# FoX attention scores by two full-height matmuls, and a projection step between the probability transposes and the value product

## The chip, the core and the metric

The kernel runs on one core of a Trainium2 chip. The time is the device time of one execution in microseconds; the median of three timed runs of the kernel before is 1479.12 us (1475.91 to 1482.52). The engines are TensorE (PE in the profile, its weight loads are PEld), VectorE (DVE), ScalarE (ACT), GpSimd (POOL) and SyncE (SP), which issues the transfers. TensorE's results go to PSUM, eight banks of 512 float32 columns on 128 partitions.

## The reference

One decoder layer on 512 tokens of width 1024, in float32: a SwiGLU half-step, a token mixer of two branches side by side, and a second SwiGLU half-step, each between norms and scaled by vectors made from a conditioning input. The change lies in the mixer's second branch, forgetting attention (FoX), with 16 heads of 64 columns:

```
def fox_attention(q, k, v, logf):
    F = jnp.cumsum(logf, axis=-1)
    ...
    def block(args):
        qi, Fi, i = args
        s = jnp.einsum('bhqd,bhkd->bhqk', qi, k).astype(jnp.float32) * scale
        s = s + Fi[..., None] - F[:, :, None, :]
        ...
        s = jnp.where(kpos[None, :] <= qpos[:, None], s, -jnp.inf)
        p = jax.nn.softmax(s, axis=-1)
        return jnp.einsum('bhqk,bhkd->bhqd', p.astype(v.dtype), v)
```

A block has 128 queries. With 512 tokens there are four of them, and the masked scores need 1, 2, 3 and 4 tiles of 128 keys.

## The kernel before

**Products in parts.** TensorE takes float32r operands, which hold fewer bits than float32. So a matrix is split into a first part and a remainder (`hi`, `lo`), and a product is the sum of three matmuls, hi·hi, hi·lo and lo·hi, into one PSUM bank (`mm3`, L192). All projections go that way: weights are loaded in pieces of 512 KB, rounded to hi by ScalarE (L155), subtracted to lo by VectorE (L156).

**Scores.** Two heads, a pair, share the 128 partitions: head e (0 or 1) has its 64 columns on half e. For a head, `qk_parts` puts the query's first part on the head's own half `n` of a tile `qx[e]` and its remainder on the other half `o`. In `kx[e]` the key's remainder is on `n` and its first part on `o`. A 128-row matmul of `qx[e]` and `kx[e]` gives hi·lo + lo·hi at once (L748), and a 64-row matmul on half `n` alone, with the key's first part `kh`, gives hi·hi (L747). Each query tile of each head takes these two, for 128, 256, 384 or 512 keys: 16 score matmuls to a pair. VectorE adds the forget bias and the mask, which GpSimd prepares from a transferred row (L731 to L737), and takes the maximum, in one instruction per tile (L751); this also frees the score's PSUM bank.

**Softmax and turn.** `fox_soft`: negated maximum (L758), exponentials with their sums on ScalarE (L760), reciprocals (L762), normalization on VectorE (L764). `fox_out`: 20 transposes of 128 x 128 into PSUM (L776), six copies to SBUF by ScalarE (L778), eight products with the values (L784), and the split of the result into parts (L198, L199).

**What sets the order.** Attention alone would leave TensorE waiting for the softmax, so projections of later pairs stand between its parts. `Fill` holds them as steps of 12 matmuls of 512 columns; `F.run(n)` takes the next n, `F.until` all up to a mark. The loop at L841 is the plan: softmax of pair p, a step, scores of pair p + 1, the steps for pair p + 2's query and key, transposes and values of pair p (`fox_out`), `evacuate()` (the parts of pair p + 2), one more step. A scheduler then orders every engine's instructions at build time, starting from this program order, and each engine runs its own list strictly in that order. A matmul that waits therefore holds back all matmuls behind it.

**Space.** SBUF has 69 units of 2 KB a partition, shared by everything but the weights (`unit()`); a pair's parts take five of them. Of the eight PSUM banks six are for long accumulations (`acc()`: projections, scores, value products, one transposed group), two for short ones (`aux()`: the other transposes). A pair's projections hold two of the six while they run.

Of the kernel before, what the change touches and what calls it, by code (L numbers as in the profile page):

```python
# [8 lines left out]
F32 = mybir.dt.float32  # L9
F32R = mybir.dt.float32r  # L10
# [3 lines left out]
ALU = mybir.AluOpType  # L14

P = 128
# [6 lines left out]
EPS = 1e-6  # L23
# [4 lines left out]
NU = 69        # 2 KiB units per partition that everything but the weight stream shares  # L28
# [3 lines left out]
NMM = 6        # PSUM banks for long accumulations; the others for short ones  # L32
LOOK = 4       # steps that weight loads run ahead
KTAIL = 6      # last contraction tiles of a down projection, taken token tile by token tile
ROWS_A = (4, 5, 5, 4)  # of a column's 8 products in the first modulation, those off VectorE
# [4 lines left out]
def tile_hybrid_layer(  # L40
# [43 lines left out]
    @contextmanager  # L84
    def in_order(last):
        # each engine issues what the block traces in the order of the trace; last: its last instructions
        start = len(nc.cur_bb.bb.instructions)
        yield
        for i in list(nc.cur_bb.bb.instructions)[start:]:
            if i.engine in last:  # L90
                after_inst(i, last[i.engine])
            last[i.engine] = i

    @contextmanager
    def not_before(last):
        # no engine issues what the block traces before its last of those
# [62 lines left out]
    class Block:  # L159
        # rows k0*128.. and columns c0.. of a weight matrix, loaded in parts of 512 KiB  # L160
# [8 lines left out]
        def fetch(self, a=0, b=None):  # L169
            # the parts that cover rows a..b, where not on the way yet  # L170
# [31 lines left out]
    def ada_acc(src):  # L202
        # silu(c) weighted sums over each partition's 8 rows of 512 columns
# [17 lines left out]
    def ada_fetch_first(ch):  # L221
        # rows of shift and scale of the first sub-layer, in space that is free at the start
# [8 lines left out]
    def ada_sum_a(us, ks):  # L231
        # the sums of the first rows of those, on ScalarE and GpSimd
# [5 lines left out]
    def ada_sum_b(us, k0):  # L238
        # of the last, on VectorE, and of both
# [11 lines left out]
    def mod_cols(shc, scc, i, ch):  # L251
        # shift and scale of sub-layer i, 256 columns of each, one column per 128
# [26 lines left out]
    def mod_gate(g, i, h, factor):  # L279
        # factor * gate * g_post as a row on all partitions, 512 columns  # L280
# [18 lines left out]
    def rstd_of(s0, s1, width):  # L299
        # (s0 + s1) / width + EPS, to the power -1/2; s0 may be absent  # L300
# [32 lines left out]
    def x_turned(tp, xn, dp, bank=aux):  # L333
        # two normalized token tiles, columns 256*dp.., transposed
# [7 lines left out]
    def make_h(tp, hs, shc, scc):  # L342
        # two token tiles: normalize, transpose, modulate, split
# [27 lines left out]
    def gu_matmuls(ps, gw, uw, hs, ks, ts, js=range(4), late=False):  # L371
        # js: gate and up of each of the two row tiles; late: with the second parts of h last
# [8 lines left out]
    def ffn(w_gu, w_dn, hs, extra, gate, after, ps=None):  # L381
        # ps: the first block's products, where they are there already
# [56 lines left out]
    for u in xT:  # L439
        nc.gpsimd.memset(u[:, 0:1], 0.0)    # takes its place ahead of the loads below  # L440
# [3 lines left out]
    with in_order(last):  # L444
# [9 lines left out]
        def norm(t):  # L454
            # into space that is for weights later
# [16 lines left out]
        def modulated(ch, a, n):  # L472
            # ahead of this and after it, the first n and the others of the next chunk's rows
# [58 lines left out]
    class Fill:  # L532
        # projections in steps of 2.6 us of tensor engine work, in order; loads run LOOK steps ahead
# [25 lines left out]
        def nat(self, c0, evac):  # L559
            # h @ w_in[:, c0:c0+512] in natural layout, by token tile  # L560
# [573 lines left out]
```

## Time and profile before

| what | value |
|---|---|
| median of 3 timed runs | 1479.12 us (1475.91 to 1482.52) |
| span of the profiled execution, first to last instruction | 1477.1 us |
| that median less that span | 2.0 us |
| TensorE busy | 1431.9 us, 97% |
| VectorE, ScalarE, GpSimd busy | 765.0, 518.4, 204.6 us |
| attention stage, first score to last value product | about 501 to 695 us |

The page gives no time of the profiled execution other than its span; the median is 2.0 us above it. Engines work side by side, so busy shares don't add up; what matters is who is waited for. Matmuls overlap in the records (one that is listed with 0.39 us is followed by the next after 0.23), so "busy" is not "at full rate", and the price of a matmul is read from start to start. The granted clock is TensorE's: 1.00 is 2.4 GHz and 0.50 is 1.2 GHz; a value between is a stretch with both.

### The profile page before, as it was taken

To read this page: it belongs to the slowest core of one execution; us is meant where nothing else is said; L and a number is where in the kernel's file an instruction comes from. 1 tells how busy PE (TensorE), PEld (TensorE's weight loads), DVE (VectorE), ACT (ScalarE), POOL (GpSimd) and SP (SyncE) were. 2 spreads that over 40 slices of the span, in tenths; PEclk is the share of its full clock that TensorE was granted. 3 is DMA by queue.
4 is the path that set the end of the run, shared out by engine and by line. 5 is a ranking of instruction groups with operands and counts; after the bars stand their busy time and mean duration, and the time that the engine had idled before them with its cause. 6 is when DMAs were issued, how large, how long until landed. Compare 5 with 4: busy or idle time off the path is not lost.

```text
span 1477.1 us, 17043 instructions
## 1 busy us (share of the span) xinstructions
PE 1431.9 (97%) x6477; PEld 1134.2 (77%) x6477; DVE 765.0 (52%) x1210; ACT 518.4 (35%) x891; POOL 204.6 (14%) x328
## 2 busy tenths in 40 slices
PE   4899999999999999999999999999999999999998
PEld 3688888878877766767888887887878888887886
DVE  6945543462265677572544565547664334346232
ACT  5332222232154353534733343433343223222121
POOL 6200000000061633340101112100050000000001
PEclk7999999999999999999999999999999999999999
DMA  9444542272337645122242222224623322335411
GB/s 322 153 140 148 159 149 86 72 242 100 87 105 217 195 138 156 37 72 61 68 131 84 72 72 64 65 73 134 221 72 96 103 87 86 100 100 171 143 58 57
DMA packets 156462, 173.35 MB, mean 117 GB/s; under 512 B 8778, under 2 KB 123574, under 8 KB 156380
## 3 DMA queue, kind: packets, MB, share of 16 engines
q1 hardware_dynamic: 156380, 172.26, 37.9%
q8 instruction: 51, 0.84, 0.2%
q14 instruction: 31, 0.25, 0.1%
HBM read 168.00 MB, written 4.23 MB: 117 GB/s over the span
## 4 chain that ended last, share of the span: by engine, by line
PE 88%; DVE 6%; ACT 2%; issue 1%; DMA 1%; POOL 1%; SPq 0%; DVEq 0%; POOLq 0%; ACTq 0%
PE mm L192 47%; PE mm L378 32%; PE mm L784 2%; PE mm L747 2%; PE mm L748 1%; PE aux L957 1%; DVE t L213 1%; PE aux L776 1%; DVE wlo L156 1%; PE aux L268 1%; ACT jk L314 1%; DMA raw<-in_w_dn_dram 1%; POOL sm L310 1%; DMA u<-in_x_dram 0%; DVE t L243 0%
## 5 line engine op out<-in xcount | busy, mean ns | idle before, releaser
L156 DVE TENSOR_TENSOR wlo<-raw,whi 128x1024 fp32r<-128x1024 f32 x218 | 271.7, 1249 | 412.4 <-ACT whi L155 404.6
L378 PE MATMUL mm<-u,whi 128*128 128x512 f32 (+1 forms) x1472 | 451.4, 390 | 10.3 <-ACT u L198 9.9
L155 ACT CAST whi<-raw 128x1024 fp32r<-128x1024 f32 x220 | 230.3, 1050 | 543.9 <-PE mm L192 301.6
L192 PE MATMUL mm<-whi,u 128*128 128x512 f32 x1216 | 390.4, 397 | 1.5 <-ACT u L198 1.5
L378 PEld LDWEIGHTS mm<-u,whi 128*128 128x128 f32 x1472 | 274.4, 190 | 75.5 <-ACT u L198 13.1
L192 PE MATMUL mm<-u,whi 128*128 128x512 f32 x896 | 292.2, 406 | 0.8 <-DVE u L984 0.8
L378 PE MATMUL mm<-u,wlo 128*128 128x512 f32 (+1 forms) x736 | 283.4, 389 | 0.0
L192 PEld LDWEIGHTS mm<-whi,u 128*128 128x128 f32 x1216 | 228.2, 188 | 54.3 <-ACT u L198 1.7
L192 PE MATMUL mm<-wlo,u 128*128 128x512 f32 x608 | 240.3, 395 | 0.0
L192 PEld LDWEIGHTS mm<-u,whi 128*128 128x128 f32 x896 | 170.2, 192 | 44.4 <-issue 2.5
L192 PE MATMUL mm<-u,wlo 128*128 128x512 f32 x448 | 179.8, 402 | 0.0
L378 PEld LDWEIGHTS mm<-u,wlo 128*128 128x128 f32 x736 | 139.7, 190 | 31.0
L192 PEld LDWEIGHTS mm<-wlo,u 128*128 128x128 f32 x608 | 114.2, 188 | 27.9
L192 PEld LDWEIGHTS mm<-u,wlo 128*128 128x128 f32 x448 | 86.1, 192 | 20.7
L307 POOL TENSOR_SCALAR sm<-ss 128x1 f32<-128x1 f32 x12 | 2.3, 191 | 666.8 <-ACT jk L314 666.8
L198 ACT CAST u<-t 128x512 fp32r<-128x512 f32 (+1 forms) x84 | 44.5, 537 | 113.8 <-DVE t L401 78.3
L213 DVE SCALAR_TENSOR_TENSOR t<-raw,csil,t 128x512 f32<-128x512 f32 x98 | 74.4, 759 | 2.7 <-DMA raw<-in_w_ada_dram 0.7
L735 POOL TENSOR_SCALAR u<-t,Ft 128x128 f32<-128x128 f32 (+1 forms) x64 | 42.6, 676 | 105.9 <-DMA t<-Fd 76.8
L400 DVE SCALAR_TENSOR_TENSOR t<-t,mm 128x512 f32<-128x512 f32 x44 | 30.1, 684 | 47.0 <-ACT t L399 47.0
L760 ACT ACTIVATE u<-u,sm 128x128 f32<-128x128 f32 (+1 forms) x64 | 35.3, 555 | 47.8 <-DVE sm L758 47.8
L399 ACT ACTIVATE t<-mm 128x512 f32<-128x512 f32 x44 | 26.1, 594 | 63.2 <-PE mm L378 63.2
L401 DVE SCALAR_TENSOR_TENSOR t<-t,mm 128x512 f32<-128x512 f32 x44 | 30.2, 687 | 30.7 <-PE mm L378 29.0
(175 smaller groups left out, 1124.1 us busy)
## 6 DMA issues: line engine op xcount, KB each, us to landing
raw<-in_w_gu_dram SPq DMA_DIRECT2D x88, 512.0 KB, 3.8
raw<-in_w_in_dram SPq DMA_DIRECT2D x64, 512.0 KB, 3.8
raw<-in_w_dn_dram SPq DMA_DIRECT2D x44, 512.0 KB, 3.8
raw<-in_w_ada_dram SPq DMA_DIRECT2D x64, 256.0 KB, 3.1
raw<-in_w_ada_dram SPq DMA_DIRECT2D x24, 512.0 KB, 3.8
u<-in_w_ada_dram SPq DMA_DIRECT2D x32, 256.0 KB, 6.6
raw<-in_w_in_dram SPq DMA_DIRECT2D x16, 256.0 KB, 3.0
t<-Fd SPq DMA_DIRECT2D x16, 256.0 KB, 4.4
```

Source lines behind the costliest of these rows:

```text
L155: nc.scalar.copy(hi, raw)
L156: (eng or nc.vector).tensor_tensor(lo, raw, hi.bitcast(F32), ALU.subtract)
L192: nc.tensor.matmul(ps, a[i], b[j], start=first and n == 0, stop=last and n == 2)
L198: nc.scalar.copy(hi, src)
L213: nc.vector.scalar_tensor_tensor(a, raw[:, j, :], csil[:, k:k + 1], a, ALU.mult, ALU.add)
L378: nc.tensor.matmul(p_[:, ts], w_[k][i][:, cs], hs[k][e][:, ts], start=ks[0] == 0 and n == 0, stop=ks[-1] == KD - 1 and n == 3 * len(ks) - 1)
L400: nc.vector.scalar_tensor_tensor(th, th, 1.0, pg, ALU.add, ALU.mult)
L401: nc.vector.scalar_tensor_tensor(th, th, 0.5, pu, ALU.mult, ALU.mult)
L735: nc.gpsimd.tensor_scalar(s_at(s, i), fb[:, 0:n], -1.0, Ft[:, i, h:h + 1], ALU.mult, ALU.add)
L747: nc.tensor.matmul(sp[:, 0:n], qx[e][es, ts], kh[es, 0:n], start=True, stop=False)
L760: nc.scalar.activation(s_at(S[e], i), s_at(S[e], i), AF.Exp, bias=nmx[e][:, i:i + 1], accum_out=rs[e][:, i:i + 1])
L784: nc.tensor.matmul(po[64 * e:64 * e + 64, j * P:T], vb[j][h // 8][:, (h % 8) * 64:(h % 8 + 1) * 64], p_at(PT[e], j), start=j == 0, stop=j ...
```

## The change

`qk_parts` builds two key tiles for each head: `kx[e]` as before, and `ky[e]`, with the key's first part on half `n` and its remainder on half `o`. The hi·hi matmul becomes a 128-row matmul of `qx[e]` and `ky[e]`, which gives hi·hi + lo·lo. The shared 128-row copy `kh` is gone; a pair's parts take six units. On ScalarE a pair has six instructions in place of three, on VectorE six as before. `fox_out` is cut in two, `fox_turn` (transposes and copies) and `fox_out` (value products), and one step of projections, taken from those ahead of the transposes, goes between them. Comments are dropped, which moves no instruction.

```diff
             def parts(q, k):
-                qx, kx, kh = (unit(F32R), unit(F32R)), (unit(F32R), unit(F32R)), unit(F32R)
-                nc.scalar.copy(kh, k)
+                qx, ky, kx = [(unit(F32R), unit(F32R)) for _ in range(3)]
                 for e in range(2):
                     n, o = halves[e], halves[1 - e]
+                    nc.scalar.copy(ky[e][n], k[n])
+                    nc.vector.tensor_tensor(kx[e][n], k[n], ky[e][n].bitcast(F32), ALU.subtract)
                     nc.scalar.activation(qx[e][n], q[n], AF.Copy, scale=scale)
                     nc.vector.scalar_tensor_tensor(qx[e][o], q[n], scale, qx[e][n].bitcast(F32),
                                                    ALU.mult, ALU.subtract)
-                    nc.vector.tensor_tensor(kx[e][n], k[n], kh[n].bitcast(F32), ALU.subtract)
-                    nc.vector.tensor_copy(kx[e][o], kh[n])
-                dst.append((qx, kx, kh))
+                    nc.vector.tensor_copy(kx[e][o], ky[e][n])
+                    nc.scalar.copy(ky[e][o], kx[e][n])
+                dst.append((qx, ky, kx))
...
             for e in range(2):
-                es, ts = halves[e], slice(i * P, (i + 1) * P)
+                ts = slice(i * P, (i + 1) * P)
                 sp = acc()
-                nc.tensor.matmul(sp[:, 0:n], qx[e][es, ts], kh[es, 0:n], start=True, stop=False)
+                nc.tensor.matmul(sp[:, 0:n], qx[e][:, ts], ky[e][:, 0:n], start=True, stop=False)
                 nc.tensor.matmul(sp[:, 0:n], qx[e][:, ts], kx[e][:, 0:n], start=False, stop=True)
...
-    def fox_out(p, state):
+    def fox_turn(state):
         S = state[0]
         PT = []
...
             PT.append(pt)
+        return PT
+
+    def fox_out(p, PT):
         po = acc()
...
         if p < 6:
-            F.until(marks[p + 2])
-        else:
-            F.run((1, 5)[p - 6])
-        fox_out(p, st[p])
+            F.until(marks[p + 2] - 1)
+        elif p == 7:
+            F.run(4)
+        PT = fox_turn(st[p])
+        F.run(1)
+        fox_out(p, PT)
         evacuate()
```

On TensorE, the end of the third pair's turn. L776 is a transpose, L784 a value product, L192 a projection; `aux` and `mm` are PSUM banks. Before:

```order
L776 MATMUL aux_4524<-ident,u_4195 128x128
L776 MATMUL aux_4524<-ident,u_4194 128x128
L784 MATMUL mm_4547<-u_4509,u_3068 64x512
L776 MATMUL aux_4537<-ident,u_4211 128x128
L776 MATMUL aux_4537<-ident,u_4210 128x128
L776 MATMUL aux_4537<-ident,u_4209 128x128 x2
L776 MATMUL aux_4543<-ident,u_4210 128x128
L776 MATMUL aux_4543<-ident,u_4209 128x128
L784 MATMUL mm_4547<-u_4528,u_3068 64x512
L784 MATMUL mm_4547<-u_4510,u_3070 64x384
L192 MATMUL mm_4595<-u_2850,whi_4383 128x512
L784 MATMUL mm_4547<-u_4529,u_3070 64x384
```

and of the changed kernel, in which the transpose is L778 and the value product L789:

```order
L778 MATMUL aux_4322<-ident,u_3976 128x128
L778 MATMUL aux_4322<-ident,u_3975 128x128
L192 MATMUL mm_4157<-u_2860,whi_4022 128x512
L192 MATMUL mm_4157<-u_2861,whi_4022 128x512
L192 MATMUL mm_4157<-u_2860,wlo_4023 128x512
L192 MATMUL mm_4157<-u_2862,whi_4022 128x512
L192 MATMUL mm_4157<-u_2863,whi_4022 128x512
L192 MATMUL mm_4157<-u_2862,wlo_4023 128x512
L192 MATMUL mm_4157<-u_2864,whi_4022 128x512
L192 MATMUL mm_4157<-u_2865,whi_4022 128x512
L192 MATMUL mm_4157<-u_2864,wlo_4023 128x512
L789 MATMUL mm_4340<-u_4288,u_3068 64x512
```

The value products stood in three pieces, between transposes and a projection; now all eight stand together (seven more follow the last row), behind nine projections.

On TensorE, the start of the fifth pair's scores. L747 is the 64-row score matmul, L748 the 128-row one; the width is the number of keys. Before:

```order
L747 MATMUL mm_4431<-u_4341,u_4337 128x128
L192 MATMUL mm_4388<-u_2858,whi_4256 128x512
L192 MATMUL mm_4388<-u_2859,whi_4256 128x512
L192 MATMUL mm_4388<-u_2858,wlo_4257 128x512
L192 MATMUL mm_4388<-u_2860,whi_4256 128x512
L192 MATMUL mm_4388<-u_2861,whi_4256 128x512
L748 MATMUL mm_4431<-u_4339,u_4337 128x128
L747 MATMUL mm_4434<-u_4341,u_4338 128x128
L747 MATMUL mm_4439<-u_4341,u_4337 128x256
L748 MATMUL mm_4439<-u_4339,u_4337 128x256
L747 MATMUL mm_4442<-u_4341,u_4338 128x256
```

and of the changed kernel, with L749 for hi·hi + lo·lo and L750 for the cross terms:

```order
L749 MATMUL mm_4451<-u_4355,u_4353 128x128
L750 MATMUL mm_4451<-u_4357,u_4353 128x128
L192 MATMUL mm_4407<-u_2858,wlo_4193 128x512
L192 MATMUL mm_4407<-u_2860,whi_4192 128x512
L192 MATMUL mm_4407<-u_2861,whi_4192 128x512
L192 MATMUL mm_4407<-u_2860,wlo_4193 128x512
L192 MATMUL mm_4407<-u_2862,whi_4192 128x512
L192 MATMUL mm_4407<-u_2863,whi_4192 128x512
L749 MATMUL mm_4454<-u_4356,u_4354 128x128
L749 MATMUL mm_4459<-u_4355,u_4353 128x256
L750 MATMUL mm_4454<-u_4358,u_4354 128x128
L750 MATMUL mm_4459<-u_4357,u_4353 128x256
```

The order of the scores is nearly the same; the first tile's second matmul comes earlier, and in the groups that stand unbroken the order does not change at all.

On ScalarE, the copies of the third pair's transposes (L778), with the exponentials of the next pair (L760). Before:

```order
L760 ACTIVATE u_4209,sm_4221<-u_4209,sm_4220 128x512
L778 COPY u_4286<-aux_4289 128x512
L778 COPY u_4287<-aux_4295 128x512
L778 COPY u_4288<-aux_4301 128x256
L778 COPY u_4305<-mm_4308 128x512
L155 CAST whi_4465<-raw_4463 128x1024
L778 COPY u_4306<-aux_4314 128x512
L778 COPY u_4307<-aux_4320 128x256
```

and of the changed kernel, where the copy is L780 and the exponential L762:

```order
L762 ACTIVATE u_4210,sm_4221<-u_4210,sm_4220 128x512
L780 COPY u_4288<-aux_4291 128x512
L780 COPY u_4289<-aux_4297 128x512
L762 ACTIVATE u_4226,sm_4237<-u_4226,sm_4236 128x128
L780 COPY u_4290<-aux_4303 128x256
L780 COPY u_4307<-mm_4310 128x512
L780 COPY u_4308<-aux_4316 128x512
L780 COPY u_4309<-aux_4322 128x256
L762 ACTIVATE u_4227,sm_4237<-u_4227,sm_4236 128x256
```

All eight exponentials of the next pair stood ahead of the copies; now four stand ahead, one between and three behind.

## Rows read from the trace of the kernel before

**Rows 1.** The page: busy us per engine; engines' shares of the chain that ended last.

```profile
PE 1431.9 (97%) x6477; PEld 1134.2 (77%) x6477; DVE 765.0 (52%) x1210; ACT 518.4 (35%) x891; POOL 204.6 (14%) x328
...
PE 88%; DVE 6%; ACT 2%; issue 1%; DMA 1%; POOL 1%; SPq 0%; DVEq 0%; POOLq 0%; ACTq 0%
```

**Rows 2.** Stages, whole attention: us, busy per engine (instructions), PEclk, DMA, GB/s.

```profile
501.00:695.00 194.00, 193.72 (x840) 133.54 (x839) 122.26 (x324) 93.47 (x228) 65.37 (x125) 0.95 0.34 99
```

**Rows 3.** Stages: score groups 501.19, 655.73; the other rows are projections.

```profile
501.19:507.53 6.34, 6.34 (x18) 3.46 (x17) 4.49 (x15) 2.03 (x3) 6.34 (x13) 0.81 0.78 225
507.53:515.25 7.72, 7.72 (x25) 5.84 (x23) 5.36 (x11) 4.15 (x11) 5.58 (x11) 0.71 0.32 114
...
545.46:551.09 5.63, 5.63 (x26) 4.47 (x25) 5.32 (x13) 3.78 (x14) 4.97 (x6) 1.00 0.31 77
566.80:573.64 6.84, 6.84 (x24) 5.39 (x23) 6.42 (x17) 4.48 (x16) 0.00 (x0) 0.77 0.50 135
614.31:621.45 7.14, 7.14 (x25) 5.63 (x24) 3.84 (x16) 4.47 (x16) 0.00 (x0) 0.76 0.00 0
655.73:662.74 7.01, 7.01 (x17) 3.77 (x17) 4.19 (x16) 0.00 (x0) 2.94 (x5) 0.71 0.00 0
662.74:666.83 4.09, 4.09 (x14) 3.20 (x13) 1.47 (x7) 2.29 (x8) 0.00 (x0) 0.65 0.01 2
```

**Rows 4.** Timeline, TensorE, scores of the fourth pair: start us, us, instruction.

```profile
561.88 0.33 PE L748 MATMUL mm<-u,u 128*128 128x128 f32 x1
562.13 0.38 PE L747 MATMUL mm<-u,u 64*128 64x256 f32 x1
...
563.38 0.44 PE L747 MATMUL mm<-u,u 64*128 64x384 f32 x1
563.75 0.44 PE L748 MATMUL mm<-u,u 128*128 128x384 f32 x1
...
565.10 0.50 PE L747 MATMUL mm<-u,u 64*128 64x512 f32 x1
565.52 0.49 PE L748 MATMUL mm<-u,u 128*128 128x512 f32 x1
```

**Rows 5.** Timeline, TensorE, fifth pair: scores of one height together (shapes merged).

```profile
585.55 0.39 PE L747 MATMUL mm<-u,u 64*128 64x128 f32 x2
...
587.52 0.67 PE L748 MATMUL mm<-u,u 128*128 128x384 f32 x3
588.12 0.44 PE L747 MATMUL mm<-u,u 64*128 64x384 f32 x1
```

**Rows 6.** Stages: transposes and value products of the third and fifth pair.

```profile
573.64:579.97 6.33, 6.33 (x39) 3.61 (x37) 3.07 (x6) 4.59 (x8) 0.00 (x0) 1.00 0.55 154
621.45:626.47 5.02, 5.00 (x38) 3.68 (x36) 0.62 (x1) 4.29 (x8) 0.00 (x0) 1.00 0.00 0
```

**Rows 7.** Timeline, TensorE, transposes of the third pair.

```profile
573.64 1.03 PE L776 MATMUL aux<-ident,u 128*128 128x128 f32 x8
574.51 0.60 PE L776 MATMUL mm<-ident,u 128*128 128x128 f32 x4
```

**Rows 8.** By line: busy us, mean ns; idle us before, and whom it waited for.

```profile
L735 POOL TENSOR_SCALAR u<-t,Ft 128x128 f32<-128x128 f32 (+1 forms) x64 | 42.6, 676 | 105.9 <-DMA t<-Fd 76.8 <-DVE u L618 22.5 <-PE aux L776 6.6
L760 ACT ACTIVATE u<-u,sm 128x128 f32<-128x128 f32 (+1 forms) x64 | 35.3, 555 | 47.8 <-DVE sm L758 47.8
L751 DVE CUSTOM_DVE_ANT_0 u<-mm,u 128x128 f32<-128x128 f32 (+3 forms) x64 | 30.1, 489 | 20.6 <-PE mm L748 18.8 <-POOL u L737 1.2 <-POOL u L735 0.3
L778 ACT COPY u<-aux 128x512 f32<-128x512 f32 (+1 forms) x40 | 18.5, 507 | 12.9 <-PE aux L776 12.4
L747 PEld LDWEIGHTS mm<-u,u 64*128 64x128 f32 x64 | 11.6, 189 | 12.6 <-issue 5.2 <-DVE sm L751 3.9 <-DVE u L764 0.5
L617 ACT ACTIVATE u<-mm 64x512 fp32r<-64x512 f32 x16 | 9.5, 595 | 16.6 <-DVE u L618 16.6
L614 ACT CAST u<-mm 128x512 fp32r<-128x512 f32 x8 | 4.7, 593 | 0.0
```

More of the change, by code (lines that the diff above doesn't have):

```diff
@@ L724, in p_at, with fox_scores @@
         return (u[0], u[1][:, 0:384], u[2], u[1][:, 384:512])[j]
-    def fox_scores(p, qx, kx, kh):
+    def fox_scores(p, qx, ky, kx):
         S, nmx, rs = [], [], []
```

## The prediction

> **What bounds the kernel now.** I read the page's busy line and the chain of waits first: TensorE is busy 97% of the span, and 88% of the chain that ended last is its work [rows 1]. So whatever shortens TensorE's own stream shortens the kernel, and any wait that enters that stream lengthens it. The change touches one stage, the attention (FoX) part. By the stage view it runs from 501 to 695 us: 194.0 us with TensorE busy for 193.7, VectorE for 122, ScalarE for 93 and GpSimd for 65 [rows 2]. The words "TensorE busy" hide two things there, and I read them from narrower stretches. First, the granted clock in the stage is 0.95, and it is 1.00 in most of it: it drops to the lower level (1.2 instead of 2.4 GHz) four times, each time during or just after a long unbroken group of sixteen score matmuls, those of the first, fourth, sixth and eighth pair of heads; the projection matmuls behind run slowly for it [rows 3]. In the other four pairs the scores are cut by projections, and no drop follows. Second, in the timeline the score matmuls start far apart for their width [rows 4].
>
> **What a score costs.** A start-to-start distance is the price of a matmul in this stream. For 64-row and 128-row ones in turn it is 0.25 us at 128 columns, 0.37 at 384 and 0.42 at 512 [rows 4]; 256 columns lie midway, 0.31. A group has each width four times: 4 x 1.35 = 5.40 us. A projection matmul of 512 columns takes 5.63 / 24 = 0.234 us in an undisturbed stretch [rows 3], and eight transposes of 128 columns start within 0.87 us, 0.109 each [rows 7]. So a score matmul pays 0.15 to 0.2 us that others don't pay, about a weight load. That this comes from the alternation, not from the scores, is in three 128-row score matmuls that happen to stand together: 0.60 us until the next start for 384 + 128 + 256 columns [rows 5], where the prices in turn give 0.93.
>
> **The change, part by part.** (a) Both score matmuls become full height, so nothing alternates within a group. At the projection's rate of 0.457 ns a column, 256 and 384 columns cost 0.117 and 0.176 us; with 0.109 and 0.234 a group costs 4 x 0.636 = 2.54 us. Gain 5.40 - 2.54 = 2.86 us, for eight groups 22.9. Against it: 64-row matmuls of the two heads lie on different halves and can run side by side; two of them together take 0.39 us [rows 5], hardly longer than one. Before, that happens three times, so 3 x 0.25 = 0.8 us of the old price wasn't paid. Left: 22.1 us.
>
> The Trainium skill speaks here against the change: "TensorE: Matmul & The Clock Gate", in the table "Why this matters for your kernels", advises to put matmuls of few rows on distinct row groups, where they run at the same time. The 0.39 us for two agrees. By that rule a full-height product throws half an array away; by the rows only three places used it, which is 0.8 us, taken off above.
>
> (b) The clock. If the dense groups no longer bring it down, the projections behind the four drops get their time back: 7.72 - 5.63 and 7.14 - 5.63 for two stretches of 24 matmuls, 6.84 - 23 x 0.234 for 23, 4.09 - 12 x 0.234 for 12, together 2.09 + 1.51 + 1.46 + 1.28 = 6.3 us [rows 3]; and the two groups that lay partly in a drop, 6.34 and 7.01 us against 5.40 [rows 3], 2.5 us. Sum 8.8. I count all of it, since a group of 2.54 us has the column rate of ordinary work.
>
> (c) The projection step between transposes and value product. Nothing is added to TensorE: the step is taken from before the transposes. A turn that is cut (value products between transposes, started as soon as one copy is there) takes 6.33 us with one projection in it, 6.10 without; a whole one takes 5.02 [rows 6]. Four turns are cut in that way, two in others, two are whole. In the new order all eight value products of a pair stand together behind some ten projections, 2.3 us, in which ScalarE's copies of 0.51 us each [rows 8] finish. Gain 4 x 1.08 = 4.3, and for the two others half of that each, an estimate: 5.4 us.
>
> (d) What is added. ScalarE loses the 128-row copy of the key (0.59 us) and gets two 64-row copies out of PSUM and two in SBUF; at the 0.59 us of the 64-row activation [rows 8] that is 1.8 us more a pair, 14 us in all, on an engine busy 93 of 194 us. VectorE's work is the same. One more buffer unit is held for each pair. None of it is on TensorE, but it is on what TensorE waits for. I bound three waits, below by nothing and not less, since (a) to (c) already count TensorE at its undisturbed prices:
> - The reductions. A score bank comes free when VectorE has reduced it; a group has 8 at 0.49 us on average, 3.9 us, against 2.54 for the matmuls. Until now VectorE waited for TensorE (18.8 us) and TensorE for it in 3.9 us [rows 8]. At most each group stretches to 4.0 us: 8 x 1.45 = 11.6. I take 5, near the wait that is there already: with four banks only the last few scores need one back.
> - The parts. Each half's chain gets two ScalarE steps longer, 1.2 us, and ScalarE already waits 16.6 us within it [rows 8]. It stands on the path where the scores come soon after the value product, and queued behind a blocked score matmul are all projections. Where 24 projections lie between, they cover it. At most 7 x 1.2 = 8.4; I take three pairs of 1.0, so 3.
> - The copies of the transposes. They now stand behind exponentials of the next pair, which wait for its reductions; without the 24 projections that stood between, only about twelve cover this. Two exponentials of 0.55 us plus the accumulator reads are 1.2 us; at most 6 pairs, 7; I take 2.
>
> Sum: 22.1 + 8.8 + 5.4 = 36.3 us off, 10 back (bounds 0 and 27), net 26.3. The profiled execution has a span of 1477.1 us, and the median of the timed runs lies 2.0 above that. 1479.1 - 26.3 = 1452.8, so I say 1453 us.
>
> **The rivals.**
> - *The clock still falls.* For it: the transposes run at 128 columns in 0.109 us, about half the projections' column rate, and a score group that waits for VectorE thins out too. Against it: all eight turns have a clock of 1.00 [rows 6], and the cut groups are thin as well. It costs the 8.8 us: 1462. The Trainium skill has a rule that speaks for this rival: "TensorE: Matmul & The Clock Gate", Part 4 on PE-mode transpose, says that transposes don't count as busy for the clock. The turns at 1.00 don't bear it out here, where other matmuls stand around them. I give 0.12.
> - *VectorE and ScalarE become the bound.* In the stretch of a pair VectorE has 122 / 8 = 15 us of work, and TensorE would be left with about 20; where the modulation sums are added it is more. All waits at their upper bounds give 1453 + 17 = 1470. For it: the 3.9 us that TensorE already waits. Against it: VectorE's idle time before the reductions is TensorE's doing [rows 8]. 0.12.
> - *Full height changes nothing*, the gap being the score's own waits on semaphores: (a) falls away, 1475, which is no change. The three together [rows 5] speak against it. 0.05.
> - *Buffers run out: slower.* GpSimd builds the bias of a pair in its buffers, 42.6 / 8 = 5.3 us, and once already stood 22.5 us for a unit that the parts gave back [rows 8]. With a sixth unit held, the bias could start only when its scores are due; TensorE would stand 5.3 us a pair, 42 us for eight: 1453 + 42 = 1495. It decides from five pairs on (5 x 5.3 is more than 26). Against it: the other idle time there is waiting for its input transfer. 0.03.
> - *No new wait at all*: 1443. 0.04.
>
> **How the numbers follow.** The forecast has 0.64. The range goes from 1443 (nothing given back) to 1468, which takes in the clock rival and most of the second and leaves out about 0.13. Within 0.5%, 7.4 us, a measurement of this kernel can't be told from no change, so faster means below 1471.7: forecast, clock, most of the second rival and the last, 0.88. Same: 0.08, of the third rival and the tail of the second. Slower: 0.04.
>
> **What would show it.** Right: score groups start their sixteen matmuls within 2.6 to 4 us where they stand together, the granted clock is 1.00 from 505 us to the end of the stage, value products stand in one block of about 2.4 us, and after the stage everything takes what it took. Wrong in (a): distances of 0.25 to 0.42 us remain between full-height scores. Wrong in (d): TensorE's idle time at the score line is put to the reductions or the parts with more than 10 us, or at the transposes to the copies. The prediction fails as a whole if the attention stage ends less than 11 us earlier.

## The result and the profile after

The kernel after takes 1453.28 us (median of four runs, 1452.12 to 1454.38) against 1477.86 us for the kernel before on the same chip: ratio 0.9832, 95% interval 0.9817 to 0.9847, that is 24.8 us off (22.6 to 27.1). Forecast were 1453 us, as 26.3 us off 1479.1, the median of three runs; the runs that the result is set against have a median 1.3 us lower. So the level fits better than the fall, which was forecast 1.5 us too large. The span of the profiled execution falls from 1477.1 to 1451.2 us.

The page after, busy time per engine and the engines' shares of the chain that ended last, against [rows 1]:

```profile
PE 1399.9 (96%) x6477; PEld 1124.3 (77%) x6477; DVE 765.7 (53%) x1210; ACT 531.4 (37%) x915; POOL 203.8 (14%) x328
...
PE 56%; DVE 4%; ACT 2%; issue 1%; POOL 1%; DMA 0%; DVEq 0%; POOLq 0%; ACTq 0%
```

TensorE has 32.0 us less to do, and the span is 25.9 us shorter: part of the work taken away came back as idle time. The shares of the chain add up to 64% after and to 99% before: the chain is followed back over a shorter part of the span, so the 56% is no fall of TensorE's part and says nothing here.

Windows of the kernel after (window; us; busy per engine with instruction counts; granted clock; DMA share; GB/s). They are the whole stage, the first and the eighth score group, the transposes behind the eighth, and one pair's value products:

```profile
501.00:669.30 168.30, 161.24 (x838) 123.07 (x836) 123.54 (x324) 104.79 (x248) 65.45 (x126) 0.98 0.38 113
501.00:505.18 4.18, 2.85 (x18) 2.31 (x16) 3.38 (x12) 2.12 (x3) 4.18 (x8) 1.00 0.52 148
630.90:638.68 7.78, 4.90 (x17) 3.83 (x17) 6.87 (x19) 2.12 (x4) 4.55 (x8) 0.74 0.14 50
638.68:642.20 3.52, 3.52 (x22) 3.51 (x20) 0.99 (x6) 1.84 (x4) 0.00 (x0) 0.60 0.00 0
563.83:566.13 2.30, 2.30 (x17) 1.06 (x16) 2.23 (x8) 2.30 (x4) 0.00 (x0) 1.00 0.93 254
```

Against [rows 2] the stage is some 25 us shorter, nearly the whole change, and TensorE is idle in it for 7 us where it was idle for 0.3. The first group falls from 6.34 us to 4.18 and runs at full clock [rows 3]. The eighth is the exception: 7.01 us before, 7.78 after, with TensorE busy for 4.9 and the clock at 0.74. This is the one place in the stage where the clock still falls; before there were four.

The scores themselves, TensorE's timeline of the fourth pair after (start, us, instruction, in brackets the idle time before), against [rows 4]:

```profile
552.87 0.30 PE L749 MATMUL mm<-u,u 128*128 128x128 f32 x1 [0.27 <-DVE u L620]
553.12 0.33 PE L750 MATMUL mm<-u,u 128*128 128x128 f32 x1
...
553.57 0.28 PE L749 MATMUL mm<-u,u 128*128 128x256 f32 x1
553.69 0.28 PE L750 MATMUL mm<-u,u 128*128 128x256 f32 x1
553.81 0.34 PE L749 MATMUL mm<-u,u 128*128 128x384 f32 x1
553.99 0.34 PE L750 MATMUL mm<-u,u 128*128 128x384 f32 x1
...
554.51 0.39 PE L749 MATMUL mm<-u,u 128*128 128x512 f32 x1
554.74 0.40 PE L750 MATMUL mm<-u,u 128*128 128x512 f32 x1
```

From start to start 256 columns take 0.12 us, 384 take 0.18 and 512 take 0.23, where before 384 took 0.37 and 512 took 0.42. The 0.25 us at 552.87 stand behind a wait for the parts of query and key; the first pair of 128 columns, at 552.27, starts 0.06 us apart.

By line in the stage after (busy us, mean ns; idle time before, and on whom), against [rows 8]; the lines answer to L735, L751 and L747 there, and L623 is new:

```profile
L737 POOL TENSOR_SCALAR u<-t,Ft 128x128 f32<-128x128 f32 (+3 forms) x52 | 33.8, 659 | 52.2 <-DMA t<-Fd 45.9 <-PE mm L789 2.9 <-PE mm L192 1.7
...
L753 DVE CUSTOM_DVE_ANT_0 u<-mm,u 128x128 f32<-128x128 f32 (+3 forms) x64 | 27.9, 485 | 2.4 <-PE mm L750 1.2 <-PE mm L749 1.0
L749 PE MATMUL mm<-u,u 128*128 128x128 f32 (+3 forms) x64 | 21.0, 346 | 6.6 <-DVE sm L753 3.0 <-DVE u L620 1.8 <-ACT u L623 1.7
...
L623 ACT CAST u<-u 64x512 fp32r<-64x512 f32 x14 | 8.7, 618 | 15.5 <-DVE u L618 15.4
```

The row of L747 in [rows 8] is that of its weight loads (PEld). The score matmul itself had no idle time in the stage before:

```profile
L747 PE MATMUL mm<-u,u 64*128 64x128 f32 (+3 forms) x64 | 26.5, 429 | 0.0
```

The wait between TensorE and VectorE has turned round: the reductions hardly wait now (2.4 us, before 20.6), and TensorE waits 6.6 us at the score line, 3.0 for reductions and 3.5 for the parts of query and key.

Summed from start to start over TensorE's stream in the two stages, the scores go from 43.2 to 30.2 us. The eight turns (first transpose to last value product, less 0.234 us for each projection in between) go from 45.9 to 40.1. All that remains, the projections, falls by 6.2. Together 25 us.

**Where the eighth group waits.** TensorE there, and VectorE from 623 us on:

```profile
630.90 0.30 PE L749 MATMUL mm<-u,u 128*128 128x128 f32 x1 [0.62 <-DVE u L620]
...
633.13 0.33 PE L749 MATMUL mm<-u,u 128*128 128x128 f32 x1 [1.66 <-ACT u L623]
...
635.53 0.69 PE L749 MATMUL mm<-u,u 128*128 128x384 f32 x1 [1.17 <-DVE sm L753]
```

```profile
623.12 0.29 DVE L894 CAST masks<-t 128x256 uint8<-128x256 f32 x1 [1.27 <-POOL t L892]
625.11 0.58 DVE L894 CAST masks<-t 128x256 uint8<-128x256 f32 x1 [1.69 <-POOL t L892]
...
629.37 0.67 DVE L618 TENSOR_TENSOR u<-mm,u 64x512 fp32r<-64x512 f32 x1
...
633.49 1.06 DVE L667 TENSOR_TENSOR u<-t,u 16x512 fp32r<-16x512 f32 x1
...
635.17 0.29 DVE L753 CUSTOM_DVE_ANT_0 u<-mm,u 128x128 f32<-128x128 f32 x1
```

L894 casts seven masks for the stage that follows. Each cast waits for GpSimd, which builds a mask in a buffer that the cast before has to give back. VectorE stands in them, and so the seventh pair's normalization and the last pair's first subtract (L618, 629.37) come late. ScalarE's second copies (L623), and the scores, wait for that subtract. L667, a small fill for that stage, then stands ahead of the first reduction (L753). Nothing of this is in the forecast, which looked at what the attention's own parts wait for.

### The profile page after: what moved, and what is told of

Read it like the earlier page. It is cut to its first block, busy times and chain, and to the rows that moved or that the text cites. A ratio compares the mean times of both kernels' runs of the same rounds, so it can differ in the third digit from the quotient of the medians.

```text
span 1451.2 us, 17081 instructions
## 1 busy us (share of the span) xinstructions
PE 1399.9 (96%) x6477; PEld 1124.3 (77%) x6477; DVE 765.7 (53%) x1210; ACT 531.4 (37%) x915; POOL 203.8 (14%) x328
## 4 chain that ended last, share of the span: by engine, by line
PE 56%; DVE 4%; ACT 2%; issue 1%; POOL 1%; DMA 0%; DVEq 0%; POOLq 0%; ACTq 0%
PE mm L192 34%; PE mm L378 16%; PE aux L964 1%; PE aux L778 1%; PE mm L789 1%; DVE wlo L156 1%; ACT u L762 1%; PE mm L749 0%; PE mm L750 0%; DVE t L213 0%; DVE u L766 0%; POOL sm L310 0%; DVE u L753 0%; DMA raw<-in_w_dn_dram 0%; ACT jk L314 0%
## 5 line engine op out<-in xcount | busy, mean ns | idle before, releaser
L156 DVE TENSOR_TENSOR wlo<-raw,whi 128x1024 fp32r<-128x1024 f32 x218 | 271.9, 1250 | 405.1 <-ACT whi L155 397.1
L378 PE MATMUL mm<-u,whi 128*128 128x512 f32 (+1 forms) x1472 | 451.5, 390 | 10.3 <-ACT u L198 9.9
L192 PE MATMUL mm<-whi,u 128*128 128x512 f32 x1216 | 390.1, 397 | 1.5 <-ACT u L198 1.5
L192 PE MATMUL mm<-u,whi 128*128 128x512 f32 x896 | 288.2, 401 | 0.8 <-DVE u L991 0.8
L192 PEld LDWEIGHTS mm<-whi,u 128*128 128x128 f32 x1216 | 228.2, 188 | 54.2 <-ACT u L198 1.7
L192 PE MATMUL mm<-wlo,u 128*128 128x512 f32 x608 | 240.3, 395 | 0.0
L192 PEld LDWEIGHTS mm<-u,whi 128*128 128x128 f32 x896 | 166.2, 188 | 39.1 <-DVE u L991 1.2
L192 PE MATMUL mm<-u,wlo 128*128 128x512 f32 x448 | 177.9, 397 | 0.0
L192 PEld LDWEIGHTS mm<-wlo,u 128*128 128x128 f32 x608 | 114.2, 188 | 28.0
L192 PEld LDWEIGHTS mm<-u,wlo 128*128 128x128 f32 x448 | 84.4, 188 | 19.7
L737 POOL TENSOR_SCALAR u<-t,Ft 128x128 f32<-128x128 f32 (+1 forms) x64 | 41.7, 661 | 95.5 <-DMA t<-Fd 89.2
L401 DVE SCALAR_TENSOR_TENSOR t<-t,mm 128x512 f32<-128x512 f32 x44 | 30.2, 686 | 31.1 <-PE mm L378 29.4
L199 DVE TENSOR_TENSOR u<-t,u 128x512 fp32r<-128x512 f32 x52 | 35.6, 689 | 16.1 <-ACT u L198 15.9
```

The lines of the kernel that those rows point to most:

```text
L156: (eng or nc.vector).tensor_tensor(lo, raw, hi.bitcast(F32), ALU.subtract)
L192: nc.tensor.matmul(ps, a[i], b[j], start=first and n == 0, stop=last and n == 2)
L199: (eng or nc.vector).tensor_tensor(lo, src, hi.bitcast(F32), ALU.subtract)
L378: nc.tensor.matmul(p_[:, ts], w_[k][i][:, cs], hs[k][e][:, ts], start=ks[0] == 0 and n == 0, stop=ks[-1] == KD - 1 and n == 3 * len(ks) - 1)
L401: nc.vector.scalar_tensor_tensor(th, th, 0.5, pu, ALU.mult, ALU.mult)
L737: nc.gpsimd.tensor_scalar(s_at(s, i), fb[:, 0:n], -1.0, Ft[:, i, h:h + 1], ALU.mult, ALU.add)
```

## The experiments

The runs' times were compared with runs of the kernel before on their own chip, so I compare ratios.

**1. Full height alone, and 2. the cut turn alone.** Each takes one half of the change back:

```diff
 # 1: after, the old loop            # 2: before, the new loop
...
-        PT = fox_turn(st[p])        +        PT = fox_turn(st[p])
-        F.run(1)                    +        F.run(1)
-        fox_out(p, PT)              +        fox_out(p, PT)
+        fox_out(p, st[p])           -        fox_out(p, st[p])
```

> The full-height scores alone: the kernel after, with the old loop in which the value product follows its own transposes and the projection step stands behind it. Theory (the terms of the prediction add up, and the turn's cut is worth its own 5.4 us): 6 us slower than after, about 1459 us, still 18 us under before; score groups as in after (2.6 to 4.2 us a pair, the eighth 7 to 8), the clock at 1.00 in all but the eighth group, and turns of 5 us in which the value products stand behind the last copies. Rival (the cut in the turn only moves the wait and is worth nothing): 1453 us, no difference from after. Rival (the whole gain is the scores' and the cut costs): under 1452 us.

> The cut turn alone: the kernel before, with its 64-row and 128-row scores, and the projection step between the transposes and the value product. Theory: 5 to 8 us under before, about 1471 us; value products of a pair in one block of 2.3 us, the score groups still 5.4 us of TensorE a pair, and the clock falling three or four times as in before, for some 6 us each. Rival (the two parts need each other, since the scores wait in the same places): within 2 us of before, 1476 to 1478 us.

Measured: full height alone 1457.37 us, ratio 0.9859 (0.9845 to 0.9874), 20.8 us under before. The cut turn alone 1475.64 us, ratio 0.9982 (0.9972 to 0.9992), 2.7 us under before (1.2 to 4.1). The two add up to 23.5, the whole change to 24.8, so they hardly need each other. The turn is worth less than forecast where it stands alone. In its trace the eight turns do fall to 40.0 us, as in the kernel after, 5.9 less than before. But the scores grow from 43.2 to 44.9 us, the eighth group to 10.1 us from first to last start, with transposes of the pair before scheduled into it:

```profile
649.51:659.59 10.08, 8.17 (x23) 4.41 (x23) 7.54 (x20) 1.09 (x2) 4.91 (x7) 0.76 0.19 57
```

That accounts for 1.7 us of the 3.2 that are missing. The rest the trace can't settle: its execution took 1473.3 us, 2.3 under the median of the twelve.

**3. Masks later.** The kernel after, with the mask block held back on VectorE and GpSimd until the attention's instructions there are issued:

```diff
+    fox_last = {}
+    for i in list(nc.cur_bb.bb.instructions):
+        if i.engine in (mybir.EngineType.DVE, mybir.EngineType.Pool):
+            fox_last[i.engine] = i
     F.until(start_b + 8)
...
-    for li, Lv in enumerate(LEVELS):
+    with not_before(fox_last):
+        for li, Lv in enumerate(LEVELS):
```

> The kernel after, with the seven masks of the next stage (21 GpSimd instructions and 7 VectorE casts) held back until the eighth pair's softmax has been issued on those engines. Theory (the eighth group is late because VectorE stands in the casts, which wait for GpSimd, ahead of this group's subtracts and reductions; the clock falls since TensorE then works only now and then): the eighth group falls from 7.8 us to 3 to 4, the clock stays at 1.00 from 505 us to the end of the stage, the transposes after it take 2.3 us in place of 3.5; 5 us under after, about 1448 us. Rival (the clock falls in the eighth group because no projection step breaks it, the casts being hidden): group at 5 to 6 us, the clock still falls for some 6 us, 1451 to 1453 us. Rival (the masks then come late for the stage that reads them): 1454 us or more.

Measured: 1448.2 us, ratio 0.9797 (0.9784 to 0.9810), 5 us under the kernel after. The eighth group and the transposes behind it:

```profile
629.96:633.05 3.09, 2.82 (x18) 2.38 (x16) 3.03 (x15) 0.00 (x0) 2.23 (x10) 1.00 0.00 0
633.05:635.56 2.51, 2.43 (x22) 2.06 (x20) 1.49 (x8) 1.73 (x4) 0.00 (x0) 1.00 0.00 0
```

The group takes 3.09 us in place of 7.78, unbroken as it was, and the clock holds. So what lowered the clock there was a group thinned out by waits, not one without a projection step. How thin it must be isn't settled: the first group of the kernel after, busy for 2.85 of 4.18 us, keeps 1.00. One point of the expectation failed: in this execution the clock falls once near the first group (503.6 us), where TensorE waits 1.5 us for a reduction.

**4. Masks later in the kernel before.** The same edit on the other kernel, to see whether before paid for the masks too.

> The kernel before with the masks held back in the same way. Theory (before had its eighth pair's parts done ahead of the casts, so that the stall there is new in the kernel after): 0 to 2 us under before, 1476.5 to 1478.5 us, the eighth group at 5.4 to 7 us and the clock still falling in it. Rival (the casts delayed before's eighth group as much): 5 us under before, 1473 us, the eighth group at 4.6 us.

Measured: 1479.11 us, ratio 1.0001 (0.9990 to 1.0012). The eighth group as it was:

```profile
656.10:663.20 7.10, 7.10 (x18) 3.79 (x18) 3.75 (x15) 0.00 (x0) 2.22 (x10) 0.71 0.00 0
```

Before, the casts were over at 649.7 us and the pair's parts began at 651.5. So the masks' 5 us are a wait that the change uncovered: its shorter stage brings the last pair to where the masks stand.

**5. The same four matmuls, in another order.** The kernel before; in each tile the two heads' 64-row matmuls first, then the two 128-row ones:

```diff
...
+            for e in range(2):
+                nc.tensor.matmul(sps[e][:, 0:n], qx[e][halves[e], ts], kh[halves[e], 0:n], start=True, stop=False)
             for e in range(2):
-                nc.tensor.matmul(sp[:, 0:n], qx[e][es, ts], kh[es, 0:n], start=True, stop=False)
-                nc.tensor.matmul(sp[:, 0:n], qx[e][:, ts], kx[e][:, 0:n], start=False, stop=True)
+                nc.tensor.matmul(sps[e][:, 0:n], qx[e][:, ts], kx[e][:, 0:n], start=False, stop=True)
```

> The same four matmuls of a tile as before in another order: the two heads' 64-row ones first, then the two 128-row ones, so that the height changes twice a tile where it changed four times; nothing else of before is changed. Theory (a change of height costs 0.15 to 0.2 us, and 64-row matmuls of different halves run side by side): a group at full clock falls from 4.6 us to 3.0 to 3.4, the stage's scores from 43 to 31, some 9 to 13 us under before, about 1467 us. Rival (a 64-row matmul is slow in itself, whoever its neighbours are): groups as before, 1478 us.

Measured: 1466.62 us, ratio 0.9911 (0.9893 to 0.9929), 13.2 us under before: half of the change's gain from the order alone. The scores of the stage take 31.6 us, before 43.2. The clock's part is in the 13.2 us too: it falls once in this stage (504.3 us), not four times, and the projections take 5.3 us less. (The profiled execution is the fastest of the six, 1461.4 us.) TensorE's timeline of the fourth pair (like ones together, x2):

```profile
556.03 0.33 PE L746 MATMUL mm<-u,u 64*128 64x128 f32 x2
556.28 0.44 PE L748 MATMUL mm<-u,u 128*128 128x128 f32 x2
...
557.40 0.44 PE L746 MATMUL mm<-u,u 64*128 64x384 f32 x2
557.77 0.62 PE L748 MATMUL mm<-u,u 128*128 128x384 f32 x2
558.22 0.40 PE L192 MATMUL mm<-u,whi 128*128 128x512 f32 x1
558.55 0.50 PE L746 MATMUL mm<-u,u 64*128 64x512 f32 x1
558.98 0.50 PE L748 MATMUL mm<-u,u 128*128 128x512 f32 x1
```

Two 64-row matmuls cost what one did: 0.25 us for the pair at 128 columns, 0.37 at 384. Two 128-row ones of 384 take 0.45, where two in turn with the others took 0.74. In the 512-column tile of this pair the matmuls came to stand in turn all the same, and there each still takes 0.43. The matmuls are those of before, so it is the change of height that costs, not 64 rows. Nor is it two matmuls in a row into one bank: those of the kernel after do that too, at 0.12 and 0.18 us. The Trainium skill says as much: "TensorEngine Tiling (Array Packing)", "Key Properties", has it that a change of tiling mode drains the engine. It gives no price; 0.15 to 0.2 us per matmul is the trace's.

**6. Half height only.** The kernel after, with each score as three 64-row matmuls on the head's own half, the heads in turn, and the parts as four instructions of 128 rows a pair:

```diff
+                qh, ql, kh, kl = [unit(F32R) for _ in range(4)]
...
+            for m, (a, c) in enumerate(((qh, kk[0]), (qh, kk[1]), (ql, kk[0]))):
+                for e in range(2):
+                    r = halves[e]
+                    nc.tensor.matmul(sps[e][:, 0:n], a[r, ts], c[r, 0:n], start=m == 0, stop=m == 2)
```

> Scores by half-height matmuls only: new loop, and each score as three 64-row matmuls (first part by first part, first by second, second by first) in one half of the rows, the pair's two heads in the two halves and issued in turn, into two banks; query and key parts then are four instructions of 128 rows a pair in place of twelve of 64 rows. Theory (what before paid for was the change of height between neighbours, not the 64 rows): a group runs at the pace of three 128-row matmuls for two heads, 1.6 us of TensorE and at most 3.5 with waits, the clock stays up, and the kernel is at after or up to 6 us under it, 1447 to 1453 us. Rival (64-row matmuls take a full pass each, and no two run side by side): 3.2 us a group plus waits, about 1.1 us more a pair than after, 1458 to 1462 us. Rival (half-filled rows let the clock fall, as it did in before's unbroken groups): falls in three or four groups, 1460 us or more.

Measured: 1452.72 us, ratio 0.9828 (0.9815 to 0.9842), not to be told from the kernel after. The group of the seventh pair:

```profile
613.63:616.12 2.49, 2.49 (x25) 1.86 (x24) 1.91 (x11) 0.00 (x0) 0.26 (x2) 1.00 0.98 218
```

24 matmuls with 7680 columns in 2.49 us are 3.1 columns a nanosecond; a projection has 2.2. So the heads' halves do run side by side, though not at twice the pace. This bears out the rule of the Trainium skill that the forecast had weighed against the change ("TensorE: Matmul & The Clock Gate", "Why this matters for your kernels": few rows on distinct row groups run at once). Here it makes three half-height passes as good as two full ones, not better. Two further findings. With fewer part instructions the eighth group takes 3.17 us although the masks stand where they stood. And half-filled rows need not lower the clock: it stays at 1.00 in seven of the eight groups. It falls at 506.6 us in the first, in which TensorE waits 1.87 us for a reduction, as it did in the full-height first group of experiment 3; so here the rows can't be told from the wait.

**7. Both of these.** Half height with the masks held back.

> Scores by half-height matmuls alone, with the masks held back. Theory (with four part instructions a pair in place of twelve, VectorE reaches the eighth group's reductions in time even with the casts in front, and holding the casts back gains nothing more): 1451 to 1453 us, as with half-height matmuls alone. Rival (the casts still cost there): 1447 us, level with the full-height kernel that holds the masks back.

Measured: 1452.13 us, ratio 0.9819 (0.9806 to 0.9832), no gain over half height alone. It fits that the masks cost only where the parts are many; full height with fewer part instructions was not run. Why this version stays 4 us above full height with the masks held back isn't settled; its projections take 99.4 us in the stage against 97.8, its scores 27.1 against 25.5.

**8 and 9. The clock alone.** The kernel before, with projection steps inside the four unbroken score groups, first one step, then one ahead of each tile but the first (the cut part takes the steps out elsewhere):

```diff
 # 8, below the tile's matmuls                    # 9, ahead of the tile's matmuls
+            if i == 2 and p in (0, 3, 5, 7):    +            if i and p in (0, 3, 5, 7):
+                F.run(1)                        +                F.run(1)
...
```

> The clock alone: the kernel before, heights as they were, with one projection step moved into each of the four unbroken score groups (first, fourth, sixth, eighth pair), behind its 256-column tiles, and taken out behind that group. Theory (the prediction's second term: the clock falls where a whole group of mixed heights runs unbroken): the clock stays at 1.00 through the stage but perhaps for one fall, score groups still 4.6 to 5.4 us, and 6 to 9 us under before, 1470 to 1472 us. Rival (mixed heights lower the clock whether or not the group is broken, or the falls cost little): within 2 us of before, 1477 to 1480 us.

> The clock again, with finer cuts: the kernel before, heights as they were, with a projection step of 12 matmuls behind each of the second, third and fourth tile's predecessors in the first, fourth, sixth and eighth pair's score groups, so that no more than four score matmuls of mixed heights stand together there; the steps are taken out of the places behind, where the second and seventh group then stand closer together than before. Theory (TensorE's clock falls only where many mixed-height matmuls stand together): no fall in the four cut groups, at most one elsewhere, and each 1 us at 1.2 GHz that goes is worth half a microsecond: 8 to 10 us less than before's 20.5 us at 1.2 GHz would cost, 1470 us. Rival (the falls stay, or move to the second and seventh group): 1474 to 1478 us, with the number of falls shown there.

Measured: one step 1475.08 us, ratio 0.9973 (0.9962 to 0.9983), 4.0 us under before, less than the 6 expected at least; the step came to stand behind the 384-column tiles, so that 12 of the 16 stayed together. Fine cuts 1472.96 us, ratio 0.9960 (0.9948 to 0.9972), 5.9 us under before (4.1 to 7.7). Of the first, the twelve scores and the step behind them, in the first and the fourth group; then of the second the fourth and the end of the sixth group:

```profile
500.77:504.98 4.21, 4.21 (x14) 2.61 (x13) 3.24 (x11) 2.03 (x3) 4.21 (x8) 0.83 0.81 227
504.98:508.79 3.81, 3.81 (x13) 2.78 (x13) 3.23 (x6) 1.88 (x2) 3.70 (x8) 0.74 0.97 307
558.39:561.74 3.35, 3.35 (x14) 2.19 (x13) 2.90 (x12) 0.00 (x0) 1.32 (x4) 0.98 0.20 78
561.74:566.13 4.39, 4.39 (x14) 3.22 (x13) 3.69 (x6) 0.13 (x1) 3.59 (x5) 0.63 0.15 43
```

```profile
558.00:575.00 17.00, 16.75 (x76) 10.69 (x74) 12.53 (x31) 5.90 (x13) 6.99 (x12) 1.00 0.53 146
610.00:622.00 12.00, 11.83 (x54) 8.35 (x55) 6.22 (x19) 3.91 (x9) 2.63 (x6) 0.86 0.29 80
```

With twelve mixed-height scores together the clock still fell in the first and the fourth group, and in the eighth, where transposes stand among them; in the sixth it didn't. With fours it stays up in three of the four groups. The one fall that is left, at 616.1 us, lies in the sixth, whose last two tiles are parted by nothing but eight matmuls of one column (L268); the fourth group has the same eight there and keeps 1.00. So how many in turn it takes isn't settled. TensorE was busy without a gap before most of these falls. That breaks in the alternation keep the clock up does hold: four falls in the stage before, one here, and a mean granted clock over the whole kernel of 0.993 to 0.997 in all six runs, against 0.981 to 0.992 in the eleven of before beside them. So the heights' alternation costs twice: by its own price, and by the clock. By the trace's clock record the stage had 20.5 us at 1.2 GHz before, 3.4 with the fine cuts, 6.8 in the kernel after. Half of the difference is what a busy engine gets back: 8.5 for the fine cuts, of which 5.9 were measured. In the trace the matmuls of the turns take 1.2 us more and the four other score groups 0.6; the rest of the difference is not accounted for.

**10 and 11. The first group.** Both hold the masks back; a projection step is put into the first group, in 10 behind the 384-column tiles, in 11 ahead of them.

```diff
             n = (i + 1) * P
...
+            if i == 2 and p == 0:     # 11; in 10 below the tile's matmuls
+                F.run(1)
...
```

> The kernel with the masks held back, and the first pair's score group broken by a projection step behind its 256-column tiles (taken out behind the group). Theory (TensorE waits 1.5 us there for the first reductions to free a bank, and a step in the gap covers it and keeps the clock up): first group from 4.2 to 5.2 us down to 2.2 to 2.8, 2 us under the kernel with the masks held back alone, 1446 us. Rival (the wait comes back a step later, at the reductions or the softmax): 1448 us.

> The kernel with the masks held back, and in the first group a projection step ahead of the 384-column tiles, where TensorE waited 1.3 us for the first reductions, held up on VectorE by a weight subtract. Theory: the wait is gone, the first group falls to 2.4 us, 1 to 1.5 us under the kernel with the masks held back alone, 1446.8 us. Rival (the same wait shows at the next reductions or at the softmax of the first pair): 1448 us.

Measured: 1447.69 us, ratio 0.9786 (0.9769 to 0.9803), and 1447.29 us, ratio 0.9782 (0.9769 to 0.9794). In 10 the step came a tile too late for the wait, which a weight subtract on VectorE (L156) causes:

```profile
502.96 1.42 DVE L156 TENSOR_TENSOR wlo<-raw,whi 128x1024 fp32r<-128x1024 f32 x1 [0.30 <-ACT whi L155]
...
504.65 0.44 PE L749 MATMUL mm<-u,u 128*128 128x384 f32 x1 [1.32 <-DVE sm L755]
```

In 11 that wait is gone, and 0.61 us of waiting for a reduction come back ahead of the last two matmuls (507.64 us). The first group's matmuls take 2.65 us, and the clock is 1.00 in the whole stage, as it is in 10. But the gain over experiment 3 is about 1 us, and the intervals overlap: not shown. The fastest version is then the full-height kernel with the masks held back, 1447 to 1448 us, 30 us under before.

## Why the prediction was right

**(a) Full-height scores, 22.1 us off, and (d) waits, 10 back.** The price was right: undisturbed groups of the kernel after take 2.49 us (fifth and seventh pair), forecast 2.54, and experiment 5 shows the cause, the change of height. The old price was put 1.7 us too high: the four groups cut by projections took 4.60 to 5.19 us, together 2.5 under four times 5.40, of which the forecast took off 0.8. At 2.49 us eight groups would take 19.9; they take 30.2, so 10.3 us came back at the scores. The size of (d) fits, its places only in part. The 3.9 us on which it put the reductions were a wait of the weight loads; the score matmuls had none (0.0 at L747), so the 5 us had less ground than it seemed. Reductions were put at 5 us and the parts at 3: TensorE's idle time at the score line is 3.0 and 3.5, and it did not pass the 10 us that would have refuted (d). But the largest piece, 5 us in the eighth group (idle time and the clock that falls with it), comes from the masks of the next stage, which no term names. Two signs of being right failed, in whole or in part: two of the three unbroken groups took 4.18 and 7.78 us, not 2.6 to 4, and the clock fell at 634.7 us. That the total came out is partly luck. The copies of the transposes were put at 2 us; TensorE waited 0.3 for them. After the stage nothing moved, as forecast: from the last value product to the end it is 782.0 us, before 782.6.

**(b) The clock, 8.8 us off.** Of it, 6.3 were the projections': they fall by 6.2, and 34 of them that started at 1.2 GHz before, in 14.1 us where the others' pace gives 8.2, account for 5.9 of it. The groups' 2.5 was too much, since the eighth keeps its fall. That a dense group alone would do was right for seven pairs. The cause was right too. That a full-height group which waits may thin out enough for a fall was named by the rival of the clock, not by the forecast, and it came true at one place out of four. The transposes, which that rival put forward, did it nowhere: in the stages before and after all falls begin among scores or just behind them, and seven of eight turns after stand at 1.00.

**(c) The turn, 5.4 us off.** The turns fall by 5.8 us in the trace, and the value products stand in one block of 2.30 us. The term was right in the stage. In the timed kernel it is smaller: 2.7 us on before's scores (1.2 to 4.1), 4.0 as the difference between experiment 1 and the kernel after. For the 4.0 the trace of experiment 1 has a reason: with full height alone four turns are whole already (5.01 to 5.07 us) where two were before, and the eight fall to 44.4 us. The cut has 4.3 left to gain. The place of a projection among transposes is not free either. The fifth pair's turn after:

```profile
579.86 0.38 PE L778 MATMUL aux<-ident,u 128*128 128x128 f32 x2
580.00 0.48 PE L192 MATMUL mm<-u,wlo 128*128 128x512 f32 x1
580.31 0.60 PE L778 MATMUL aux<-ident,u 128*128 128x128 f32 x4
```

This projection, alone between transposes, takes 0.31 us from start to start, not 0.234; the 96 in the eight turns take 0.266 on average.

**The rivals.** VectorE and ScalarE did not become the bound: 7 us of idle TensorE in a stage of 168. Full height did change something (experiment 5). Buffers did not run out: GpSimd's 22.5 us for a unit that the parts gave back [rows 8] are not in its row after (L737), where the input's transfer is the wait. That no wait would come at all was refuted as well; without the masks the kernel still stays 4 to 5 us above the 1443 of that rival.

## What to carry over

Where TensorE is the bound, read matmuls from start to start: a price that depends on the neighbour (here on a change of row height) can in part be taken off by order alone (here 13 of 25 us), before any recomputation. When a stage gets shorter, look at what is queued at its end for the next stage on the engines that are not the bound, for it will now stand in the way. And a term for waits that comes out in sum should be checked place by place, since here half of it lay where nobody had looked.

## What was not expected of the hardware

The clock went down to 1.2 GHz while TensorE never stood idle, among or just behind twelve or sixteen matmuls of alternating heights (501.19 to 507.53 us before: busy throughout, 0.81). It did so in most such groups, not in all, and in seven of eight groups of half-height matmuls side by side it stayed at 1.00. Two 64-row matmuls on different halves cost the price of one next to 128-row neighbours (0.25 us at 128 columns), but a whole group of them ran at 1.4 times the columns of full-height work, not at twice.
